# Background sums of a transformer-like layer, ordered behind the weight tile that precedes them in the transfer order

## The chip, the cores and the metric

The kernel runs as one program on one core of a Trainium2 chip. The metric is the device time of one execution in microseconds (us), as the median of three runs. The profile shows one execution engine by engine: PE is TensorE (matrix multiplication; PEld are its weight loads), DVE is VectorE, ACT is ScalarE, POOL is GpSimd, SP is SyncE, which here issues the large transfers. Each engine runs its own instructions strictly in the order in which they were built, and waits on semaphores for the others.

## The reference

One layer (DEPTH is 1) on 256 latent tokens of width 2048, with 256 context tokens, all in float32:

- `mod = silu(c) @ w_mod + b_mod` gives six rows of 2048: shift, scale and gate for each of two sub-layers. Context tokens use `silu(c_ctx)`.
- Token mixer: `h = modulate(rms_norm(x))`, one projection `h @ w_in` (11264 columns), a convolution branch, a gated recurrence with 8 heads in both directions, a projection of each branch, sigmoid gates, `w_out`, and `x + ga_m * rms_norm(y)`.
- MLP: `modulate(rms_norm(x))`, `square(relu(h @ w1)) @ w2` with 8192 hidden columns, and `x + ga_f * rms_norm(...)`.

What matters here: of `w_mod`, the first two rows (shift and scale of the mixer) are needed at once. The other four (the mixer's gate, shift and scale of the MLP, the MLP's gate) are needed much later, and the kernel computes them in the background, on VectorE rather than on TensorE.

## The kernel before

All weights come as tiles of 128 x 1024 float32 (512 KB). To keep float32 precision on TensorE, each weight tile is split into two parts: ScalarE writes `whi`, a rounded copy (line 119), and VectorE writes `wlo`, the rest (line 120). TensorE then multiplies `whi` and `wlo` with the split activations. A tile that is used this way is called a weight tile below; making `whi` and `wlo` is its preparation, and `wlo` is its second part.

The class `Stream` holds one list of all tiles in the order of use. `fetch` issues the transfers from SP, strictly in list order, into a rotation of five raw buffers (`RAWS`); the transfer of a tile waits until the tile that held its buffer has been read for the last time. `prepare` takes the next tile of the list. For a weight tile it allocates one of four pairs of `whi` and `wlo` (`AHEAD`) and makes the two parts; a pair comes free when TensorE has used it, so preparation runs at most four tiles ahead of TensorE.

Between weight tiles stand 128 background tiles, also of 512 KB, each with a function `fn`. `prepare` calls it and returns; such a tile has no `whi` or `wlo`. There are two kinds, and both are one VectorE instruction over the raw tile, called a sum below:

- `dots` (line 924), 64 tiles of `wmt`: multiplies the tile with the row `silu(c)` and adds up along the row.
- `gemv` (lines 909 and 911), 64 tiles of `wm1`: adds the tile, times one value per partition, to `gacc`. After 16 tiles the generator `gain_row` adds a bias (954), splits the result into `gpart` (231), lets TensorE add it up (966) and stores a gain row (968).

Where background tiles stand in the list: two behind each tile of the second half of the first context projection; one or two behind every second weight tile from there through the recurrence heads and the convolution's inputs; none behind the first 52 tiles of the gate projections, then one behind every fourth; one behind every second tile in the two branch projections (`who`, `wpw`) and in most of `wo`; one behind every sixth in the MLP.

Two things set the order on VectorE. The Python program is written in list order, and `pump` interleaves steps of background generators (the recurrence heads, the convolution). A scheduler then builds each engine's list from the program, by its own model of when an instruction's inputs are there; it may move an instruction past others that do not depend on it. `tc.issue_after(ins)` adds a constraint for that scheduler: what is recorded inside the block on the engine of `ins` stands behind `ins` in that engine's list. It adds no semaphore. The list `kn.los` holds the `wlo` instructions made so far, in list order.

A recurrence head runs through levels. On a level TensorE multiplies (1043) what ScalarE copied to `left` (1032), VectorE stores the result under a mask (`sc`, 1050), scales two halves of `x` (1058, 1059) and a decay tile `fg` (1061), and from these `left` is copied for the next level.

The projections called `tokens` (lines 253 to 255) work in groups: four banks of PSUM are filled over all weight tiles of the group, but the last three tiles (`LAST`) are taken bank by bank, so that the banks can be emptied one after the other. The three pairs of `whi` and `wlo` therefore come free almost together, at the end of the group. Emptying is lines 729 (`who`), 737 and 738 (`wpw`) on VectorE and 718 (gates) on ScalarE.

Of the kernel before, what the change touches and what calls it, by code (L numbers as in the profile page):

```python
# [49 lines left out]
class Stream:  # L50
# [49 lines left out]
    def prepare(self):  # L100
        self.fetch_to(1)
        ap, fn, paged = self.items[self.done]
        self.done += 1
        raw = self.raws.popleft()
        kn = self.kn
        nc = kn.nc
        if fn is not None:
            fn(raw)
            return
        if paged:  # L110
            hi, lo = (kn.page(F32R, "wpage")[:, :TW] for i in range(2))
        else:
            hi = kn.wp.tile([P, TW], F32R, name="whi", tag="whi", bufs=AHEAD)
            lo = kn.wp.tile([P, TW], F32R, name="wlo", tag="wlo", bufs=AHEAD)
        with ExitStack() as after:
            for ins in self.behind[0] if self.behind else ():
                after.enter_context(kn.tc.issue_after(ins.ins))
            self.behind = self.behind[1:]
            nc.scalar.activation(out=hi, in_=raw, func=AF.Copy)  # L119
            kn.los.append(nc.vector.tensor_tensor(lo, raw, hi.bitcast(F32), op=ALU.subtract))  # L120
        self.ready.append((hi, lo))
# [1148 lines left out]
```

## Time and profile before

| | us |
|---|---|
| median of 3 runs | 1670.3 |
| lowest, highest | 1669.09, 1670.92 |
| the profiled execution: its time | 1668.67 |
| its span | 1666.9 |
| PE busy in the span | 1628.6 |
| DVE busy | 1123.8 |
| ACT busy | 772.5 |

The span runs from the first to the last instruction of the program; the time of the execution is 1.77 us longer. Busy times of engines overlap. A row of a wait gives what waited, for whom, the sum, the number of times and the longest. A row of the timeline gives start, length, engine, line, operation, the tiles written and read, and in brackets the idle time before it and what ended it. In windows, each engine has its busy time and instruction count, and PEclk is the granted clock of TensorE as a share of full speed.

### The profile page before, as it was taken

What the parts mean: (1) busy time and instruction counts of PE and PEld (TensorE: products, weight loads), DVE (VectorE), ACT (ScalarE), POOL (GpSimd) and SP (SyncE); (2) the same over time, 40 slices, a digit from 0 to 9 for tenths busy, and PEclk for the clock granted to TensorE, in tenths of its full rate; (3) what the DMA queues carried; (4) which work ended last, traced back from release to release, by engine and by line L of the source; (5) the groups of instructions that cost most, each with busy time, mean ns of one, the idle gap of its engine ahead of it and who ended that gap; (6) DMA issues with size and microseconds to landing.
All of it is one profiled execution on the core that took longest, in us unless ns stands there. A gap on an engine that the chain in (4) does not pass through costs nothing.

```text
span 1666.9 us, 22131 instructions
## 1 busy us (share of the span) xinstructions
PE 1628.6 (98%) x8378; PEld 1366.7 (82%) x8378; DVE 1123.8 (67%) x1558; ACT 772.5 (46%) x1075; POOL 8.1 (0%) x18
## 2 busy tenths in 40 slices
PE   5999999999999999999999999999999999999997
PEld 3668888888888888778788898888888888888886
DVE  5446687887877888867887756456565665566555
ACT  4222444344554444643345655446543455345543
POOL 0000000000000000000000000000000000000000
PEclk9999999999999999999999999999999999999999
DMA  9997863543566555678888366677667666666553
GB/s 377 394 371 277 301 208 122 179 151 114 185 205 202 182 189 191 223 253 292 287 276 282 125 228 230 212 240 232 216 209 229 235 221 215 223 218 200 184 193 116
DMA packets 103338, 374.47 MB, mean 225 GB/s; under 512 B 11584, under 2 KB 11584, under 8 KB 103232
## 3 DMA queue, kind: packets, MB, share of 16 engines
q1 hardware_dynamic: 101952, 368.86, 65.1%
q0 software_dynamic: 1280, 4.21, 0.8%
q8 instruction: 65, 1.06, 0.3%
q14 instruction: 41, 0.34, 0.1%
HBM read 370.93 MB, written 2.10 MB: 224 GB/s over the span
## 4 chain that ended last, share of the span: by engine, by line
PE 81%; DVE 8%; DMA 6%; issue 2%; ACT 2%; SPq 0%; DVEq 0%; ACTq 0%
PE bank L179 19%; PE bank L246 18%; PE bank L255 10%; PE bank L254 10%; PE bank L253 10%; PE bank L248 9%; DMA raw<-wm 5%; DVE wlo L120 3%; PE bank L1043 2%; DVE gacc L911 1%; DMA raw<-wmt 1%; ACT whi L119 1%; DMA x<-ctx 1%; DVE raw L924 0%; ACT turned L891 0%
## 5 line engine op out<-in xcount | busy, mean ns | idle before, releaser
L120 DVE TENSOR_TENSOR wlo<-raw,whi 128x1024 fp32r<-128x1024 f32 x490 | 594.6, 1222 | 316.6 <-ACT whi L119 311.9
L119 ACT ACTIVATE whi<-raw 128x1024 fp32r<-128x1024 f32 x490 | 515.0, 1059 | 592.3 <-PE bank L255 304.8
L246 PE MATMUL bank<-h,whi 128*128 128x512 f32 x1280 | 322.2, 393 | 0.0
L246 PEld LDWEIGHTS bank<-h,whi 128*128 128x128 f32 x1280 | 230.3, 189 | 41.4
L179 PE MATMUL bank<-h,whi 128*128 128x512 f32 (+1 forms) x768 | 210.7, 362 | 1.8 <-ACT whi L119 1.0
L253 PE MATMUL bank<-whi,hidh 128*128 128x512 f32 x500 | 194.6, 389 | 0.0
L254 PE MATMUL bank<-wlo,hidh 128*128 128x512 f32 x500 | 194.6, 389 | 0.0
L255 PE MATMUL bank<-whi,hidl 128*128 128x512 f32 x500 | 194.5, 389 | 0.0
L248 PEld LDWEIGHTS bank<-h,wlo 128*128 128x128 f32 x1280 | 174.6, 190 | 12.6
L254 PE MATMUL bank<-wlo,h 128*128 128x512 f32 x448 | 175.6, 392 | 4.3 <-DVE wlo L120 4.2
L248 PE MATMUL bank<-h,wlo 128*128 128x256 f32 x1280 | 178.4, 282 | 0.0
L253 PE MATMUL bank<-whi,h 128*128 128x512 f32 x448 | 175.5, 392 | 0.0
L255 PE MATMUL bank<-whi,h 128*128 128x512 f32 x448 | 175.0, 391 | 0.0
L179 PEld LDWEIGHTS bank<-h,whi 128*128 128x128 f32 x768 | 132.1, 190 | 24.6 <-issue 5.9
L179 PE MATMUL bank<-h,wlo 128*128 128x512 f32 (+1 forms) x384 | 135.6, 355 | 0.0
L911 DVE SCALAR_TENSOR_TENSOR gacc<-raw,silu_c,gacc 128x1024 f32<-128x1024 f32 x60 | 77.0, 1283 | 66.4 <-DMA raw<-wm 66.4
L255 PEld LDWEIGHTS bank<-whi,hidl 128*128 128x128 f32 x500 | 93.8, 188 | 19.6
L254 PEld LDWEIGHTS bank<-wlo,hidh 128*128 128x128 f32 x500 | 93.9, 188 | 19.5
L253 PEld LDWEIGHTS bank<-whi,hidh 128*128 128x128 f32 x500 | 93.9, 188 | 19.2
L254 PEld LDWEIGHTS bank<-wlo,h 128*128 128x128 f32 x448 | 84.5, 189 | 23.3 <-DVE wlo L120 6.0
L255 PEld LDWEIGHTS bank<-whi,h 128*128 128x128 f32 x448 | 84.4, 188 | 17.6
L253 PEld LDWEIGHTS bank<-whi,h 128*128 128x128 f32 x448 | 84.5, 189 | 17.2
(206 smaller groups left out, 1617.7 us busy)
## 6 DMA issues: line engine op xcount, KB each, us to landing
raw<-w SPq DMA_DIRECT2D x256, 512.0 KB, 4.2
raw<-wi SPq DMA_DIRECT2D x172, 512.0 KB, 4.0
raw<-wm SPq DMA_DIRECT2D x80, 512.0 KB, 4.3
raw<-wmt SPq DMA_DIRECT2D x64, 512.0 KB, 4.2
rawpage<-wm SPq DMA_DIRECT2D x48, 512.0 KB, 9.2
raw<-wo SPq DMA_DIRECT2D x32, 512.0 KB, 4.7
raw<-who SPq DMA_DIRECT2D x16, 512.0 KB, 4.7
raw<-wpw SPq DMA_DIRECT2D x16, 512.0 KB, 5.1
```

Source lines behind the costliest of these rows:

```text
L119: nc.scalar.activation(out=hi, in_=raw, func=AF.Copy)
L120: kn.los.append(nc.vector.tensor_tensor(lo, raw, hi.bitcast(F32), op=ALU.subtract))
L179: ins = fn(*args, **kw)
L246: nc.tensor.matmul(bank, w[0][:, cut(i)], x(k)[2], start=(k == 0), stop=False)
L248: nc.tensor.matmul(bank[:, T:], w[1][:, cut(i)], x(k)[0], start=False, stop=(k == nk - 1))
L253: nc.tensor.matmul(out, x[0], w[0], start=first, stop=False)
L254: nc.tensor.matmul(out, x[0], w[1], start=False, stop=False)
L255: nc.tensor.matmul(out, x[1], w[0], start=False, stop=last)
L911: nc.vector.scalar_tensor_tensor(acc, raw, s, acc, op0=ALU.mult, op1=ALU.add)
L1043: nc.tensor.matmul(ps[:, b * P:(b + 1) * P], w, r, start=True, stop=True)
```

## The change

The call of a background tile's function is put into a block that orders it behind the last `wlo` made so far, that is, behind the second part of the weight tile that precedes it in the list. No instruction is added or taken away, and no size, buffer or transfer is changed. The file becomes two lines longer, so that line 120 is 122 after the change, 911 is 913, and so on.

```diff
@@ -105,7 +105,9 @@
         kn = self.kn
         nc = kn.nc
         if fn is not None:
-            fn(raw)
+
+            with kn.tc.issue_after(kn.los[-1].ins):
+                fn(raw)
             return
         if paged:
             hi, lo = (kn.page(F32R, "wpage")[:, :TW] for i in range(2))
```

The built programs show how this moves instructions. The first place is VectorE at the change from the projection `who` to `wpw`, where the group's four banks are emptied (`gate`). Before:

```order
L911 SCALAR_TENSOR_TENSOR gacc<-raw,silu_c,gacc 128x1024
L120 TENSOR_TENSOR wlo<-raw,whi 128x1024
L729 TENSOR_TENSOR gate<-bank,gate 128x512 x2
L911 SCALAR_TENSOR_TENSOR gacc<-raw,silu_c,gacc 128x1024
L729 TENSOR_TENSOR gate<-bank,gate 128x512
L120 TENSOR_TENSOR wlo<-raw,whi 128x1024 x2
L729 TENSOR_TENSOR gate<-bank,gate 128x512
L120 TENSOR_TENSOR wlo<-raw,whi 128x1024 x2
```

And with the change:

```order
L913 SCALAR_TENSOR_TENSOR gacc<-raw,silu_c,gacc 128x1024
L122 TENSOR_TENSOR wlo<-raw,whi 128x1024
L731 TENSOR_TENSOR gate<-bank,gate 128x512 x3
L122 TENSOR_TENSOR wlo<-raw,whi 128x1024
L913 SCALAR_TENSOR_TENSOR gacc<-raw,silu_c,gacc 128x1024
L122 TENSOR_TENSOR wlo<-raw,whi 128x1024
L731 TENSOR_TENSOR gate<-bank,gate 128x512
L122 TENSOR_TENSOR wlo<-raw,whi 128x1024
```

The sum that stood between the emptying of the second and the third bank now stands behind the first `wlo` that follows the third bank.

The second place is VectorE in the levels of the first recurrence head (its tile is `x_1824`). Before:

```order
L1061 TENSOR_TENSOR fg<-fg 128x256
L924 SCALAR_TENSOR_TENSOR raw,dot<-raw,silu_row 128x1024
L1050 COPY_PREDICATED sc<-masks,bank 128x2x128
L1058 TENSOR_TENSOR x_1824<-x_1824,fg 128x96x4
L1059 TENSOR_TENSOR x_1824<-x_1824,fg 128x96x4
L120 TENSOR_TENSOR wlo<-raw,whi 128x1024
L1061 TENSOR_TENSOR fg<-fg 128x128
L1010 TENSOR_SCALAR fg<-fg,lbm,lb 128x512
L1050 COPY_PREDICATED sc<-masks,bank 128x2x128
```

And with the change:

```order
L1063 TENSOR_TENSOR fg<-fg 128x256
L1052 COPY_PREDICATED sc<-masks,bank 128x2x128
L1060 TENSOR_TENSOR x_1824<-x_1824,fg 128x96x4
L1061 TENSOR_TENSOR x_1824<-x_1824,fg 128x96x4
L122 TENSOR_TENSOR wlo<-raw,whi 128x1024
L1063 TENSOR_TENSOR fg<-fg 128x128
L926 SCALAR_TENSOR_TENSOR raw,dot<-raw,silu_row 128x1024 x2
L1052 COPY_PREDICATED sc<-masks,bank 128x2x128
```

Sums that stood singly on several levels now stand as a pair behind a `wlo`. Counted over the whole of VectorE's two lists, 107 of the 128 sums stood ahead of the `wlo` of the weight tile before them, by one to four `wlo`; with the change none does, 124 stand right behind it and the first four one or two `wlo` later, where they stood before. The order on SP and POOL is unchanged. On TensorE a few small multiplications of the heads, of the gain rows and of the transposes ahead of `wo` move by one to six rows, and on ScalarE some copies change places with neighbours.

## The prediction

> **What bounds the kernel now.** I read the busy times first, then TensorE by stage, then who it waits for.
>
> ```profile
> span 1666.9 us, 22131 instructions
> PE 1628.6 (98%) x8378; PEld 1366.7 (82%) x8378; DVE 1123.8 (67%) x1558; ACT 772.5 (46%) x1075; POOL 8.1 (0%) x18
> ```
>
> TensorE is busy 1628.6 of 1666.9 us. The change gives it no less to do, so it can win only what TensorE loses: the 38.3 us in which it is idle, and time in which its clock is down. By stage (columns: length, then busy time of PE, PEld, DVE, ACT, POOL; clock; DMA share; GB/s):
>
> ```profile
> 200.00:480.00 280.00, 278.59 (x1545) 241.09 (x1544) 220.62 (x407) 121.56 (x227) 1.45 (x2) 1.00 0.50 166
> 680.00:960.00 280.00, 271.97 (x1290) 225.72 (x1288) 210.08 (x251) 142.56 (x209) 4.32 (x8) 0.99 0.73 248
> 960.00:1640.00 680.00, 679.96 (x3546) 585.03 (x3547) 403.41 (x404) 340.80 (x423) 2.09 (x4) 1.00 0.66 217
> ```
>
> The MLP (960 to 1640) has nothing to win: 0.04 us idle. The heads (200 to 480) have 1.41 us, and the stretch from the end of the gates to the end of `wo` (680 to 960) has 8.03 us and a clock below 1.00. The rest of the 38.3 lies in the start and the tail, where no sum moves. Who is waited for:
>
> ```profile
> PE bank L254 <- DVE wlo L120: 4.2, 3, 1.9
> PE bank L966 <- DVE gpart L231: 1.8, 2, 1.5
> PE bank L1043 <- ACT left L1032: 1.3, 3, 0.5
> ```
>
> ```profile
> DVE gacc L911 <- DMA raw<-wm: 66.4, 50, 3.7
> DVE raw L924 <- DMA raw<-wmt: 20.2, 18, 2.3
> ```
>
> VectorE stands 86.6 us in front of sums whose transfer has not landed. All that is behind such a sum waits too, though its own inputs may be there. That costs something only where TensorE is short of a `wlo`, and the first rows say where to look: three times, 4.2 us.
>
> **The change, part by part.** Nothing is added, so durations stay: a sum 1.28 us, a `wlo` 1.2, a `whi` 1.06. Only places on VectorE's list move.
>
> *First stall.* VectorE, ScalarE and TensorE around 742:
>
> ```profile
> 735.16 2.40 DVE L120 TENSOR_TENSOR wlo<-raw,whi 128x1024 fp32r<-128x1024 f32 x2
> 741.26 1.28 DVE L911 SCALAR_TENSOR_TENSOR gacc<-raw,silu_c,gacc 128x1024 f32<-128x1024 f32 x1 [3.70 <-DMA raw<-wm]
> 742.47 2.35 DVE L120 TENSOR_TENSOR wlo<-raw,whi 128x1024 fp32r<-128x1024 f32 x2
> ```
>
> ```profile
> 737.97 1.06 ACT L119 ACTIVATE whi<-raw 128x1024 fp32r<-128x1024 f32 x1 [1.66 <-PE bank L255]
> ```
>
> ```profile
> 741.62 0.39 PE L255 MATMUL bank<-whi,h 128*128 128x512 f32 x1
> 741.85 0.39 PE L253 MATMUL bank<-whi,h 128*128 128x512 f32 x1
> 743.74 0.50 PE L254 MATMUL bank<-wlo,h 128*128 128x512 f32 x1 [1.51 <-DVE wlo L120]
> ```
>
> Matmuls start every 0.23 us. The `whi` is ready at 739.03, but VectorE idles until 741.26 for a transfer of a tile that comes later in the list, sums until 742.47, and only then makes the `wlo`. With the sum behind it, that `wlo` runs from about 739.1 to 740.3, and TensorE asks for it at 742.08: 1.8 us to spare. The idle 1.5 us goes. **Term 1: -1.5** (no less, since the spare is larger than what moved things could cost here; at most 1.66, the step 741.85 to 743.74 less 0.23).
>
> *Second stall*, at the group end shown in the order rows:
>
> ```profile
> 791.16 1.22 DVE L120 TENSOR_TENSOR wlo<-raw,whi 128x1024 fp32r<-128x1024 f32 x1
> 792.29 1.28 DVE L729 TENSOR_TENSOR gate<-bank,gate 128x512 f32<-128x512 f32 x2
> 795.86 1.28 DVE L911 SCALAR_TENSOR_TENSOR gacc<-raw,silu_c,gacc 128x1024 f32<-128x1024 f32 x1 [2.29 <-DMA raw<-wm]
> 797.07 0.68 DVE L729 TENSOR_TENSOR gate<-bank,gate 128x512 f32<-128x512 f32 x1
> 797.67 2.35 DVE L120 TENSOR_TENSOR wlo<-raw,whi 128x1024 fp32r<-128x1024 f32 x2
> ```
>
> ```profile
> 792.81 2.96 ACT L119 ACTIVATE whi<-raw 128x1024 fp32r<-128x1024 f32 x3 [5.74 <-PE bank L255]
> ```
>
> ```profile
> 796.69 0.39 PE L253 MATMUL bank<-whi,h 128*128 128x512 f32 x1
> 798.94 0.64 PE L254 MATMUL bank<-wlo,h 128*128 128x512 f32 x1 [1.86 <-DVE wlo L120]
> ```
>
> Three pairs come free together, three `whi` follow back to back from 792.81, and their `wlo` are wanted at once. In the new order a third bank is emptied ahead of the `wlo`; it was waited for behind the sum before, so its own time is not seen. Banks end nine matmuls (2.1 us) apart and the three `whi` start when the tile is last read, about 1.4 us before the last bank ends, so bank three is out at most 0.7 us after 792.81; with its 0.68 the `wlo` still ends by 795.4, and TensorE asks at 796.92. The sum then comes between the first and the second `wlo`: the second ends by 795.4 + 1.28 + 1.2 = 797.9, while TensorE needs it 12 matmuls later, at 799.7. The fourth bank's emptying and the third `wlo` end by 799.8, against 802.4. **Term 2: -1.9** (0.7 if the third bank came 2.3 us later than I place it; 2.0 at most).
>
> *The clock behind it.* Windows of 2 us, same columns:
>
> ```profile
> 798.00:800.00 2.00, 1.06 (x3) 0.87 (x4) 2.00 (x3) 0.00 (x0) 0.00 (x0) 0.79 1.03 416
> 800.00:802.00 2.00, 2.00 (x7) 1.54 (x6) 2.00 (x4) 1.06 (x1) 0.00 (x0) 0.50 0.93 344
> 802.00:804.00 2.00, 2.00 (x9) 1.65 (x8) 0.89 (x1) 0.65 (x1) 0.00 (x0) 0.86 0.99 313
> ```
>
> The clock falls to half right behind the longest stall and is back by 804. Lost: 2 x (0.21 + 0.50 + 0.14) = 1.7 us. Nothing follows the shorter stall at 742. I take it that without the stall the clock stays: **term 3: -1.7** (0 if the drop has another cause). [...]
>
> *The third wait on a `wlo`*, at the end of the gates:
>
> ```profile
> 698.34 0.50 PE L254 MATMUL bank<-wlo,h 128*128 128x512 f32 x1 [0.88 <-DVE wlo L120]
> ```
>
> ```profile
> 690.54 1.22 DVE L924 SCALAR_TENSOR_TENSOR raw<-raw,silu_row 128x1024 f32<-128x1024 f32 x1 [0.96 <-DMA raw<-wmt]
> 692.84 1.74 DVE L333 RECIPROCAL lnmu<-lnmu 128x256 f32<-128x256 f32 x1
> ```
>
> From 690.54 VectorE has no pause until the late `wlo`. Taking the sum and its wait out of that run gives 2.2 us, and the new order has this sum behind the `wlo`; but the reciprocal waits for the convolution's own chain, which may not come earlier. Between 0 and -0.9, I take **term 4: -0.6**.
>
> *The gain row:*
>
> ```profile
> 830.16 0.51 PE L966 MATMUL bank<-gpart,ones_r 128*128 128x512 f32 x1 [1.45 <-DVE gpart L231]
> ```
>
> The chain sum, bias, split, matmul has the same length, its last sum is now later in VectorE's list, and TensorE's rows for it move one to three matmuls (0.2 to 0.7 us) later. TensorE itself arrives sooner. Between +0.7 and -1.4, **term 5: -0.4**.
>
> *The heads.* 20.2 us of waits for `wmt` go, which lie between levels. Against that, pairs of sums (2 x 1.22) now stand on one level. A level takes 12 matmuls and four small ones, about 3.2 us, and where VectorE is ahead it waits:
>
> ```profile
> 241.16 0.45 DVE L1050 COPY_PREDICATED sc<-masks,bank 128x256 f32<-128x256 uint8 x1 [1.09 <-PE bank L1043]
> 242.44 1.22 DVE L120 TENSOR_TENSOR wlo<-raw,whi 128x1024 fp32r<-128x1024 f32 x1
> ```
>
> The level's own work is 1.3 us (241.16 to 242.44) and `fg`, about 0.3. A level with two sums and a `wlo` is 1.6 + 2.4 + 1.2 = 5.2 us of VectorE: 2.0 too long, less that 1.1. By the order lists six levels are like that, three before, so up to 3 x 0.9 = +2.7; the other end is -1.3, all that line 1043 waits for. The ends nearly cancel: **term 6: 0**.
>
> *What a later sum holds up.* A raw buffer is freed later, and SP's next transfers with it.
>
> ```profile
> raw<-wm SPq DMA_DIRECT2D x80, 512.0 KB, 4.3
> raw<-wpw SPq DMA_DIRECT2D x16, 512.0 KB, 5.1
> ```
>
> With a sum behind every second tile, five buffers hold 3.3 weight tiles, 3.3 x 2.7 = 9 us of TensorE; transfer, `whi` and `wlo` take 5.1 + 1.1 + 1.2 = 7.4. **Term 7: 0**, as long as transfers stay under about 6.7 us.
>
> Sum: -1.5 - 1.9 - 1.7 - 0.6 - 0.4 = -6.1. The profiled execution took 1668.67 (span 1666.9), 1.6 below the median of 1670.3; I take the sum off the median: **1664.2 us**.
>
> **The rivals.**
>
> *A. As summed, in size or part:* terms 1 and 2 alone with the clock give 5.1; 1665.2. All at their best (1.66 + 2.0 + 1.7 + 0.9 + 1.4 + 1.3) give 9.0; 1661.3.
>
> *B. The heads and the gain row give it back:* terms 1 to 3 hold, but +2.7 and +0.7 come on top: -1.7, 1668.6. For it speaks that pairs of sums are new; against it that the waits on `wmt`, which no order of instructions shows, go away there.
>
> *C. The bubbles stay:* three pairs freed at once need 3 `whi` and 3 `wlo`, whatever the order, and only four pairs exist. Then terms 1 to 3 vanish, 1669.7 with term 4. [...] Against it: at 737.97 and 792.81 the `whi` were made in time, and the pair was free.
>
> *D. Slower: transfers come late.* From 720 to 920 each sum holds its buffer until the preceding `wlo` is done, so that at a group end the next transfers start after the burst. If they then take over about 6.7 us, TensorE runs dry at each of the six group ends, by about 2.0 us plus 1.7 of half clock: 6 x 3.7 less the 5.7 of terms 1 to 4 = +16.5, 1686.8. It decides from transfers of 6.7 us; 5.1 is the median there, and `x` is loaded beside them around 784 to 800.
>
> *E. The change does nothing:* excluded for most sums by the order lists (107 of 128 move), open only if VectorE's waits reappear in other places; 1670.3.
>
> **How the numbers follow.** Runs of this kernel differ by up to 1.8 us; what is within 0.2% (3.3 us) counts as no change. A 0.72, B 0.12, C 0.08, D 0.06, E 0.02. Faster means below 1667.0: nearly all of A, 0.71; slower is D, 0.06; the rest 0.23. The range holds A, with a run's spread at its lower end, and B with most of C up to 1669.3: 1660.3 to 1669.3; A's own is 1661 to 1667.
>
> **What would show it.** Right: the waits of the sums on DMA fall from 86.6 to under 15 us; the wait of line 254 (then 256) on `wlo` from 4.2 to under 0.5; the clock at 1.00 from 790 to 810; PE idle from 680 to 960 about 4 instead of 8.0 us. Terms 5 and 6 are read from the waits of the gain row's matmul and of the `left` level. It would be wrong if new waits of `whi` on `raw` appear between 720 and 920 (D), or if TensorE still waits for `wlo` at group ends with no sum in front (C).

## The result, and the profile after

The changed kernel takes 1659.85 us (median of 6 executions, 1658.71 to 1660.90), the kernel before beside it 1669.69 us (6 executions, 1667.99 to 1672.97). The ratio is 0.9941, with a 95% interval from 0.9931 to 0.9952: faster, by 0.6%. Measured again beside the last experiments, the ratio was 0.9932 (0.9915 to 0.9948); one execution of the kernel before, of 4227 us, is left out there. The forecast was 1664.2 us with a range from 1660.3 to 1669.3; the time lies 0.45 us under its lower end. The direction and the places were right, the size was too small. The profiled pair went from 1668.67 to 1659.94 us, its span from 1666.9 to 1658.2.

The same three stages as before, in the profile after; its program runs up to 8.7 us ahead, so that the same stretch of time holds slightly later work (length, then busy time of PE, PEld, DVE, ACT, POOL; clock; DMA share; GB/s):

```profile
200.00:480.00 280.00, 279.36 (x1550) 241.75 (x1550) 219.87 (x408) 122.05 (x227) 1.46 (x2) 1.00 0.50 165
680.00:960.00 280.00, 277.05 (x1355) 232.60 (x1354) 215.50 (x254) 146.59 (x213) 4.33 (x8) 1.00 0.72 253
960.00:1640.00 680.00, 680.00 (x3516) 583.79 (x3516) 399.92 (x402) 336.96 (x421) 2.10 (x4) 1.00 0.65 215
```

TensorE's idle time falls from 1.41 to 0.64 us in the heads and from 8.03 to 2.95 us between the gates and `wo`, and the clock there is 1.00 instead of 0.99. The MLP had nothing to win and won nothing. Who TensorE still waits for, of the rows that concern the change:

```profile
PE bank L968 <- ACT gpart L233: 1.0, 1, 1.0
PE bank L1045 <- ACT left L1034: 0.5, 1, 0.5
```

The row of line 256 and `wlo` (254 before, 4.2 us) is gone; one wait for a gain row and one for `left` remain. And the waits for transfers:

```profile
DVE raw L926 <- DMA raw<-wmt: 0.2, 1, 0.2
```

```profile
ACT whi L121 <- DMA raw<-wpw: 18.2, 10, 5.3
ACT whi L121 <- DMA raw<-wo: 15.4, 12, 3.9
ACT whi L121 <- DMA raw<-who: 15.1, 9, 2.7
ACT whi L121 <- DMA raw<-w: 8.6, 5, 2.4
```

VectorE's 86.6 us in front of sums are now 0.2. ScalarE has taken over part of it: for `wpw`, `wo`, `who` and `w` it waits 57.3 us in all, where these rows of the kernel before add up to 6.8:

```profile
ACT whi L119 <- DMA raw<-wo: 3.8, 3, 1.9
ACT whi L119 <- DMA raw<-who: 2.0, 1, 2.0
ACT whi L119 <- DMA raw<-w: 1.0, 1, 1.0
```

The transfers are not quicker (the median from issue to landing is 4.7 us for `wm` and 5.8 for `wpw`, against 4.3 and 5.1 before); the engine that meets them first has changed. ScalarE's wait shows no cost on TensorE, which waits for a `whi` once for 1.0 us in both kernels; my reading is that behind the wait stands the next `whi`, which comes later in the list anyway. VectorE's wait did cost at a few places, where a `wlo` whose tile had already landed stood behind the sum and TensorE wanted it (1.51 us in front of 743.74 and 1.86 us in front of 798.94 in the kernel before).

Where the time went, in the profiled pairs. I took the start of the n-th matmul in each trace, subtracted that of the kernel before, and read the difference at the boundaries of the stages (us; the last three columns are experiments, told below):

| stage, in the time of the kernel before | forecast | after | after, second profile | dots alone | gemv alone | two sums |
|---|---|---|---|---|---|---|
| start, to 215 | 0 | +0.1 | 0.0 | +1.9 | +0.5 | -0.4 |
| heads and convolution inputs, to 679 | 0 (term 6) | -1.0 | -1.0 | -1.0 | -0.1 | 0.0 |
| end of the gates, to 733 | -0.6 (term 4) | -1.1 | -1.1 | -1.1 | 0.0 | 0.0 |
| first stall, to 780 | -1.5 (term 1) | -1.8 | -1.8 | -0.4 | -1.8 | -1.8 |
| second stall and clock, to 823 | -3.6 (terms 2, 3) | -3.8 | -3.5 | +1.7 | -3.7 | -3.6 |
| gain rows, to 952 | -0.4 (term 5) | -1.1 | -1.3 | -0.1 | -0.8 | -0.7 |
| MLP and end | 0 | 0.0 | 0.0 | 0.0 | 0.0 | 0.0 |
| span | -6.1 | -8.7 | -8.8 | +0.9 | -5.8 | -6.5 |

The second profile is that of the run called "after, again" in the table of experiments. The start changes by chance: it lies between -1.3 and +1.9 us in the kernels whose start is the same, so its row is not an effect of the edits.

At the first stall VectorE's timeline of the changed kernel reads:

```profile
737.02 1.23 DVE L122 TENSOR_TENSOR wlo<-raw,whi 128x1024 fp32r<-128x1024 f32 x1 [1.50 <-ACT whi L121]
738.16 1.28 DVE L913 SCALAR_TENSOR_TENSOR gacc<-raw,silu_c,gacc 128x1024 f32<-128x1024 f32 x1
739.75 1.23 DVE L122 TENSOR_TENSOR wlo<-raw,whi 128x1024 fp32r<-128x1024 f32 x1 [0.30 <-ACT whi L121]
```

Each wait is now one on a `whi` that has just been made, and no sum waits. At the second:

```profile
790.06 1.23 DVE L122 TENSOR_TENSOR wlo<-raw,whi 128x1024 fp32r<-128x1024 f32 x1 [1.08 <-ACT whi L121]
791.21 1.28 DVE L913 SCALAR_TENSOR_TENSOR gacc<-raw,silu_c,gacc 128x1024 f32<-128x1024 f32 x1
792.40 1.22 DVE L122 TENSOR_TENSOR wlo<-raw,whi 128x1024 fp32r<-128x1024 f32 x1
793.54 0.68 DVE L731 TENSOR_TENSOR gate<-bank,gate 128x512 f32<-128x512 f32 x1
794.14 1.21 DVE L122 TENSOR_TENSOR wlo<-raw,whi 128x1024 fp32r<-128x1024 f32 x1
795.27 1.28 DVE L913 SCALAR_TENSOR_TENSOR gacc<-raw,silu_c,gacc 128x1024 f32<-128x1024 f32 x1
```

The group's three `wlo` and the sum between them run nearly without a break. TensorE is busy without a gap. The clock reads 1.00 from 38.97 us to 1653.47 us in this trace; the window in which it was 0.50 before:

```profile
800.00:802.00 2.00, 2.00 (x11) 1.65 (x10) 1.93 (x3) 0.52 (x2) 0.00 (x0) 1.00 0.91 311
```

### The profile page after: what moved, and what is told of

Same layout as the page of the kernel before. It is cut to its first block, busy times and chain, and to the rows that moved or that the text cites. A ratio compares the mean times of both kernels' runs of the same rounds, so it can differ in the third digit from the quotient of the medians.

```text
span 1658.2 us, 22135 instructions
## 1 busy us (share of the span) xinstructions
PE 1626.7 (98%) x8378; PEld 1366.0 (82%) x8378; DVE 1122.5 (68%) x1558; ACT 772.5 (47%) x1075; POOL 8.1 (0%) x18
## 4 chain that ended last, share of the span: by engine, by line
PE 92%; DMA 4%; ACT 2%; DVE 2%; issue 1%; SPq 0%; DVEq 0%; ACTq 0%
PE bank L181 19%; PE bank L248 18%; PE bank L257 14%; PE bank L256 14%; PE bank L255 14%; PE bank L250 9%; PE bank L1045 2%; DMA raw<-wpw 1%; ACT whi L121 1%; DMA rawpage<-wm 1%; DMA raw<-wf 1%; DMA x<-ctx 0%; DVE wlo L122 0%; ACT turned L893 0%; PE bank L1076 0%
## 5 line engine op out<-in xcount | busy, mean ns | idle before, releaser
L255 PE MATMUL bank<-whi,h 128*128 128x512 f32 x448 | 174.7, 391 | 0.0
L257 PE MATMUL bank<-whi,h 128*128 128x512 f32 x448 | 174.3, 390 | 0.0
L181 PE MATMUL bank<-whi,h 128*128 128x512 f32 x256 | 83.1, 400 | 3.2 <-ACT h L233 3.2
```

The source lines that it names most:

```text
L181: ins = fn(*args, **kw)
L255: nc.tensor.matmul(out, x[0], w[0], start=first, stop=False)
L257: nc.tensor.matmul(out, x[1], w[0], start=False, stop=last)
```

## The experiments

The theory: a sum that waits for its own transfer holds up what stands behind it in VectorE's list, and at two group ends that is the `wlo` which TensorE needs next; two instructions carry most of the gain. Against it stood rival C (too few buffers), rival D (transfers late), and the question of what the 64 `dots` are worth.

| kernel | us | before, beside it | ratio, 95% interval |
|---|---|---|---|
| dots alone ordered | 1669.38 | 1670.60 | 0.9982 (0.9967 to 0.9996) |
| gemv alone ordered | 1664.06 | 1670.60 | 0.9944 (0.9927 to 0.9961) |
| two sums ordered | 1664.33 | 1670.87 | 0.9958 (0.9941 to 0.9975) |
| before, six raw buffers | 1679.23 | 1670.60 | 1.0043 (1.0029 to 1.0056) |
| after, six raw buffers | 1665.47 | 1670.02 | 0.9966 (0.9956 to 0.9977) |
| after, four raw buffers | 1677.34 | 1670.60 | 1.0028 (1.0014 to 1.0041) |
| after, gain rows two steps later | 1671.83 | 1670.02 | 1.0011 (1.0002 to 1.0020) |
| order behind the last wlo but one | 1659.30 | 1670.02 | 0.9937 (0.9919 to 0.9954) |
| order behind the last but two | 1661.75 | 1670.87 | 0.9947 (0.9928 to 0.9966) |
| last but one, first gain row a step later | 1659.51 | 1670.87 | 0.9932 (0.9915 to 0.9948) |
| after, again | 1659.47 | 1670.87 | 0.9932 (0.9915 to 0.9948) |
| after, with pauses of TensorE (one execution) | 1736.42 | 1670.02 | none |

The ratio on record and its interval are taken over the single executions; the ratio lies up to 0.2% from the quotient of the two medians beside it (for the `gemv` alone that is 0.9961).

### Half of the change: dots alone, gemv alone

```diff
-            with kn.tc.issue_after(kn.los[-1].ins):
+            with kn.tc.issue_after(kn.los[-1].ins) if fn.__defaults__ and len(fn.__defaults__) == 2 else ExitStack():
```

> Only the sums of wmt (the dot products, which lie in the projections of the context, the recurrence heads and the gates up to about 700 us) are ordered behind the preceding wlo; the sums of wm1 stay free. If each place pays by itself, as the two traces read: the heads 0.9 us and the end of the gates 1.1 us, so about 2 us below the kernel before (ratio 0.9988), with the stalls at 742 and 797 and the clock drop still there. If the gain is one thing, that VectorE as a whole has less to wait for, these 64 of 128 sums bring nearer half of the 9.8 us, 0.997.

```diff
-            with kn.tc.issue_after(kn.los[-1].ins):
+            with kn.tc.issue_after(kn.los[-1].ins) if len(fn.__defaults__) == 3 else ExitStack():
```

> Only the sums of wm1 (from about 710 us on) are ordered; the dot products stay free. Place by place: the stall at 742 (1.8 us), the one at 797 with the clock (3.8) and the gain rows (1.1) go, about 6.7 us below the kernel before, ratio 0.996; waits of these sums on transfers near 0, those of the dot products still about 20 us. Half and half would be 0.997.

The two halves split by stage in the table above. Ordering the `dots` gives what the changed kernel gains in the heads and at the end of the gates (-2.1 us). Behind them it gains nothing, and in this profile loses 1.2: the `gemv` sums still wait 75.9 us, and TensorE still waits for `wlo` in the projections, in part at other places (1.04 us ahead of 774 where the kernel before has 1.51 ahead of 744, then 2.95 ahead of 800 and 1.10 ahead of 824). By the timed runs it is worth 0.04 to 0.33%. Ordering the `gemv` gives the two stalls, the clock and part of the gain rows, 0.4 to 0.7%.

With the `dots` alone the second stall is even longer, 2.95 us, and yet the clock stays. TensorE there:

```profile
796.71 0.39 PE L255 MATMUL bank<-whi,h 128*128 128x512 f32 x1
800.05 0.50 PE L256 MATMUL bank<-wlo,h 128*128 128x512 f32 x1 [2.95 <-DVE wlo L122]
```

I come back to this row under the clock.

### Two instructions of 128

```diff
-            fn(raw)
+            with kn.tc.issue_after(kn.los[-1].ins) if fn.__defaults__ in ((0, 3, 0), (0, 12, 0)) else ExitStack(): fn(raw)
```

> Only two of the 128 sums are ordered: those that VectorE waited in front of at 741 and 796 us. The other sums of the same accumulation follow them, so VectorE's list changes between about 740 and 830 us and nowhere else; the lists of ScalarE, GpSimd and SyncE are those of the kernel before. If the two stalls and the half clock behind the second are what these sums cost (terms 1 to 3), the two steps of 1.8 and 3.8 us go as in the changed kernel and nothing else: 4.5 to 6 us less than before, 1664 to 1666 us, ratio 0.9965 to 0.9975, and in the trace the heads (200 to 480) and the end of the gates (680 to 703) as before. If the gain needs the order of all sums (transfers start in step with the list), less than 2 us, ratio above 0.9985.

Measured: 1664.33 us, inside the first range by time; the ratio, 0.9958, is a little below the one expected. By stage the profile agrees: nothing in the heads, nothing at the end of the gates, -1.8 and -3.6 us at the two stalls. The windows of this kernel in the three stages from the end of the gates on:

```profile
680.00:705.00 25.00, 24.06 (x110) 19.51 (x109) 20.66 (x28) 17.30 (x24) 0.00 (x0) 1.00 0.67 214
705.00:760.00 55.00, 55.00 (x246) 45.52 (x245) 37.45 (x44) 29.77 (x42) 1.17 (x2) 1.00 0.73 251
760.00:812.00 52.00, 51.81 (x229) 42.56 (x229) 39.60 (x38) 18.37 (x18) 2.11 (x4) 1.00 0.91 337
```

The 0.94 us in front of the late `wlo` at the end of the gates is still there (first row), the stalls at 742 and 797 are not. The sums still wait for transfers, 53.4 us for `wm` and 18.8 for `wmt`. So the waits of the sums are not themselves the cost: 72 of 86.6 us may stay, if those two do not stand in front of a `wlo` that is wanted. Terms 1 to 3 are shown by this run. Two sums were ordered, but eleven moved: nine neighbours between 741 and 814 us add to the same `gacc` and follow them, by one to three `wlo`.

### Buffers instead of order

```diff
-NPAGE = 30
+NPAGE = 29
-RAWS = 5
-FETCH = 13
+RAWS = 6
+FETCH = 14
```

Once in the kernel before, once in the changed one:

> The old order with six raw buffers instead of five (and 29 pages instead of 30 to make room; one more transfer is issued ahead at the start). If the bubbles come from too few buffers, a sixth lets transfers run one tile further ahead and the sums' waits on transfers fall well below 86 us, the time to about 1663. If they come from the order, the scheduler moves the sums one wlo further ahead with the sixth buffer (its list shows 45 of them four wlo ahead and 13 five), the sums still wait for their transfers, and the time stays within 2 us of the kernel before.

> The new order with six raw buffers (and 29 pages). If transfers are in time with five, nothing changes: 1659 to 1661. In the new order whi waits 18 us for wpw, 15 for wo and 15 for who, against 0 to 4 before; a sixth buffer should take most of these waits away, and if they cost TensorE anything the time falls below 1659.

A sixth raw buffer does not help the kernel before, it makes it slower. Its waits:

```profile
PE bank L254 <- DVE wlo L120: 6.6, 10, 1.4
```

```profile
DVE gacc L911 <- DMA raw<-wm: 84.1, 53, 4.7
DVE raw L924 <- DMA raw<-wmt: 23.5, 18, 4.3
```

The sums wait 107.6 us instead of 86.6, and TensorE ten times for a `wlo` instead of three. Most of the 0.43% is lost elsewhere: at 90 us TensorE stops for 3.64 us and the clock halves for 6.8 us, presumably since this edit also takes a page away and lengthens the prefetch; the changed kernel with six buffers has the same stop (3.64 us at 90 us) and loses 6 us there too. So the two are to be compared with one another: 0.9966 against 1.0043, a ratio of 0.9923. The order is worth as much with six buffers as with five, and more raw buffers do not replace it. No run added pairs of `whi` and `wlo`, which rival C had named; C falls by the run with two ordered sums, where both stalls are gone with the same four pairs.

```diff
-RAWS = 5
-FETCH = 13
+RAWS = 4
+FETCH = 12
```

> The new order with four raw buffers instead of five. By the margin worked out in the prediction, four buffers hold 2.7 weight tiles, 7.3 us of TensorE, where transfer, whi and wlo take 7.4: TensorE should run short of a tile at the group ends between 720 and 920 us and wait for whi on transfers, some 5 to 20 us slower than the new order with five, 1665 to 1680. If a held buffer costs nothing because transfers run far ahead, the time stays at about 1660.

With four buffers the changed kernel is slower than the kernel before. ScalarE's waits:

```profile
ACT whi L121 <- DMA raw<-wi: 56.5, 31, 5.4
ACT whi L121 <- DMA raw<-w: 40.3, 24, 3.7
ACT whi L121 <- DMA raw<-wo: 28.1, 20, 4.9
```

The trace is 14.8 us longer than that of the changed kernel: 6.5 us are lost before 215 us, in the start, and 7.8 us between 763 and 915, where the `gemv` sums stand and TensorE now waits for `wlo` seven times and for `whi` twice (4.8 us). The clock stays at 1.00 there. This is rival D, at about half its price, and one buffer away. With five, the margin of term 7 holds, though the 57.3 us of waits say that it is used.

### How far ahead a sum may stand

```diff
-            with kn.tc.issue_after(kn.los[-1].ins):
+            with kn.tc.issue_after(kn.los[-2].ins):
```

> The sums are ordered behind the wlo before the last one, so each may stand one wlo ahead of the new place (99 of 128 do, by the list). If what costs is that a wlo waits behind a transfer that comes later in the list, some of the waits come back: sums wait 20 to 50 us in all, and the time lies between, 1661 to 1665. If one wlo ahead is still hidden by the four pairs, it is as fast as the new order, 1660.

One `wlo` further ahead costs nothing: 1659.30 us. The sums wait 11.6 us in this kernel, less than I expected, and ScalarE's waits for `wpw`, `wo` and `who` are 20.5 us, against 48.7 in the changed kernel. With `kn.los[-3]`:

> Each sum is ordered behind the wlo three tiles before instead of the last one, which lets the scheduler put sums up to two wlo earlier. If what counts is only that no sum stands in front of a wlo whose transfer comes before its own by more than VectorE's slack, some waits of the sums on transfers return (15 to 40 us in sum) and the time stays within 2 us of the changed kernel, 1658 to 1662. If the place behind the preceding wlo is itself needed, the stalls at group ends return and the time is 1663 to 1668.

1661.75 us, inside the first range near its upper end, and 2.3 above the changed kernel on the same chip, a little more than the 2 us expected; the two intervals overlap. The sums wait 33.2 us (31.8 for `wm`, 1.4 for `wmt`). In its profile 1.3 us are lost in the start, and behind the start it gains 8.7 us, as much as the changed kernel (8.8). So the place behind the very last `wlo` is not needed. The kernel before, whose sums run ahead by up to four, has the stalls; three alone was not run.

### The gain rows

```diff
         yield None
         yield None
+        yield None
+        yield None
         row = self.grow[i, h] = self.page(F32, "gain_row")[:, :TW]
```

> The new order, with the four small matmuls of a gain row recorded two steps of the background pump later. In the new order's trace TensorE waits 1.0 us for gpart at 820 us. With two more steps (two weight tiles, 5.4 us) gpart is there, so about 1 us less than the new order, 1658.9; no gain if the wait only moves to another place.

The wait of the first gain row is gone, as meant, but the kernel loses about 12 us at another place:

```profile
PE bank L876 <- DVE y L799: 6.8, 1, 6.8
```

The multiplications of the second row now run at 925.74, and what the last step of `wo` makes of it on VectorE is wanted at once by TensorE's next transposes. From 930.73, inside the stop, the clock is at half for 17 us:

```profile
930.73:934.15 3.42, 0.55 (x3) 0.55 (x4) 2.67 (x8) 2.88 (x9) 0.00 (x0) 0.50 0.00 0
934.15:947.80 13.65, 13.65 (x65) 13.30 (x63) 6.53 (x14) 4.14 (x12) 0.00 (x0) 0.50 0.12 38
```

Only the first row, by one step, together with the order one ahead:

```diff
+        if (i, h) == (0, 0):
+            yield None
         row = self.grow[i, h] = self.page(F32, "gain_row")[:, :TW]
```

> Sums one wlo ahead, and the matmuls of the first gain row alone written one step of its generator later. In the changed kernel TensorE waits 1.0 us for this row at 820 us. If it is only written too early, the 1.0 us goes and nothing is late behind it, since the forced end of this row at the end of its group is one wlo away: 1657.5 to 1659.5, about 0.8 us under the changed kernel. If it comes too late as both rows did when two steps were added, the wait moves to the group end: 1663 to 1672, with a wait of 3 to 7 us behind 820.

The wait of this row is gone from the trace, and a wait of 0.6 us for a `wlo` at 804 is new. The 0.8 us that I expected are not there: the time, 1659.51 us, is that of the changed kernel beside it (1659.47):

> The changed kernel beside the three others on one chip: 1659 to 1661 us, ratio to before 0.993 to 0.995. Its spread should stay near 2 us where the kernel before spreads over 7 us and more, if the second stall of the kernel before costs the clock in some executions and not in others.

None of the versions beats the changed kernel by an amount that these runs can tell.

### The clock

The same kernel with 18 pauses in the MLP: TensorE's list gets a small multiplication, and then a transpose of a tile that GpSimd fills in one to eight steps first. It is added work; nothing of the computation is left out.

```diff
+        with self.tc.issue_after(behind.ins):
+            ps = self.bank()
+            nc.tensor.matmul(ps[:, :P], self.ones_r, self.ones_r, start=True, stop=True)
+        nc.scalar.copy(out=self.held[:, :P], in_=ps[:, :P])
+        for _ in range(times):
+            nc.gpsimd.memset(self.held[:, :cols], 1.0)
+        with self.tc.issue_after(behind.ins):
+            return nc.tensor.transpose(out=ps[:, :P], in_=self.held[:, :P], identity=self.v["ident"])
```

> The new order, and in the down projections of the first three quarters of the MLP eighteen added pauses of TensorE: a small matmul, a copy of its result on ScalarE, one to eight memsets on POOL, and a transpose for which TensorE waits. The pauses should last about 1 to 6 us. If the clock falls after a pause of some 2 us, as at 797 in the kernel before, pauses from about 2 us on are followed by 3.4 us at half clock, and those below about 1.7 us are not. If only a pause of a whole 3.4 us or more does it, those of 2 to 3 us keep the clock at 1.00, and the drop at 799 had another cause.

Seventeen of the pauses came out between 1.50 and 5.04 us; at the other one TensorE waited for a gain row instead (0.57 and 0.84 us). Length alone does not sort them: after one of 2.67 us the clock halved, after one of 3.62 us it did not, and after another of 3.62 us it did. What sorts them is a grid. In the kernel before, the half clock at 799.14 begins 764.58 us after the one at the start (34.56), and that is 224.00 times 3.4133 us; it lasts 3.413 us, one step. In the kernel with pauses every half clock up to 1540 us begins a whole number of such steps behind the first (352, 357, 369, 378, ...), and in all 14 traces it lasts 1, 2 or 5 whole steps, the one at the very end of a program aside. So I cut the traces on this grid. Windows of the kernel with pauses, in pairs: a window with a pause, and the one behind it (the second number is TensorE's busy time, the one ahead of the last two the clock):

```profile
1250.10:1253.51 3.41, 1.10 (x6) 0.93 (x7) 1.90 (x2) 0.00 (x0) 2.08 (x4) 1.00 0.68 229
1253.51:1256.92 3.41, 3.41 (x10) 2.65 (x9) 0.00 (x0) 0.00 (x0) 0.00 (x0) 0.50 0.53 198
```

```profile
1437.83:1441.24 3.41, 1.43 (x8) 1.16 (x8) 1.23 (x1) 1.21 (x2) 0.62 (x2) 1.00 0.89 284
1441.24:1444.65 3.41, 3.41 (x10) 2.65 (x9) 0.00 (x0) 0.29 (x1) 0.00 (x0) 0.50 0.45 157
```

```profile
1263.75:1267.16 3.41, 1.58 (x8) 1.12 (x6) 1.92 (x2) 1.21 (x2) 0.53 (x2) 1.00 0.70 261
1267.16:1270.58 3.42, 1.64 (x8) 1.39 (x9) 0.46 (x1) 0.00 (x0) 1.55 (x4) 1.00 0.53 177
```

The first two windows are idle for 2.31 and 1.98 us, and half clock follows. The first pause of 3.62 us is cut into 1.84 and 1.78, and none follows; the second has 2.94 us in one window. The stall of 2.95 us with the `dots` alone is cut in the same way:

```profile
795.50:798.92 3.42, 1.59 (x8) 0.98 (x6) 1.95 (x3) 0.28 (x1) 0.00 (x0) 1.00 0.80 231
798.92:802.33 3.41, 2.28 (x10) 1.87 (x11) 3.41 (x4) 0.26 (x1) 0.00 (x0) 1.00 1.03 363
802.33:805.74 3.41, 3.41 (x17) 2.81 (x16) 2.17 (x3) 1.86 (x2) 0.00 (x0) 1.00 0.91 342
```

And the kernel before, whose second stall lay wholly in one window:

```profile
795.73:799.14 3.41, 1.55 (x7) 0.97 (x7) 3.28 (x4) 0.04 (x1) 0.00 (x0) 1.00 0.84 302
799.14:802.56 3.42, 3.42 (x9) 2.67 (x9) 3.42 (x4) 1.06 (x1) 0.00 (x0) 0.50 0.96 356
```

Over the 14 traces, between the start and the tail, all 11 windows at full clock with at least 1.98 us of idle time are followed by half clock, and 29 of 30 with 1.0 to 1.84 us are not. Between them lie the 1.86 of the kernel before, with half clock, and a 1.92 without. The exception is a window of the kernel with pauses that was idle for 1.44 us (from 1233.03) and is followed by half clock; it is the one with the two waits for a gain row, and I have no explanation for it. So in these traces the boundary lies near 1.9 us of 3.41, somewhat over half a window. Eight of the 11 windows are from the one kernel with pauses.

## Why the prediction was too small

**Terms 1 to 3 were right.** They were forecast at -5.1 and measured -5.6 (-1.8 and -3.8). The kernel with two ordered sums shows that the place of these two is the cause. The 0.5 is arithmetic: I took idle times from the bracket, but a matmul takes 0.39 us where the next one starts after 0.23, so a stop costs 0.16 more than the idle time in front of the next matmul, and the matmul that ends it is followed after 0.34 instead of 0.23 us (743.74 to 744.08). The steps between starts had shown most of it (1.66 for the first stall, which I kept only as the upper bound).

**Term 3** (-1.7) held in the profiled pair. The other branch of the expectation for the kernel with pauses, that only a pause of a whole 3.4 us or more costs the clock, is not what the runs showed: a window of 3.41 us with 1.98 us of idle time was followed by half clock. But the row alone said less than I took from it: the 1.86 us of the kernel before lie between 1.84 and 1.92 that cost nothing elsewhere, and neither did the 2.95 us of the `dots` kernel. The windows begin 0.42 us past a whole number of steps from the program's first instruction in the trace of the kernel before, and 1.42 us in that of the changed kernel. I infer from it that whether an execution of the kernel before pays the 1.7 us depends on where a window begins; one execution of it was profiled, and it paid.

**Term 4** (-0.6) was mis-sized: -1.1. I had kept half for the reciprocal, which might not come earlier. It did come earlier (690.83 against 692.84, of which 0.9 is the gain of the heads), the sum now stands behind the first of the two late `wlo`, and the whole stop of 0.88 + 0.16 us is gone.

**Term 5** (-0.4) was mis-sized: -1.1 to -1.3, near the end of its bounds that I called -1.4. The longer of the first row's waits fell from 1.45 to 0.98 us, and the wait of 0.31 us before the second row, at 919.95, disappeared, with the 0.16 that a stop costs besides.

**Term 6** (0) is the step that failed in its reasoning. I counted up to +2.7 for levels with two sums, and let it cancel the gain. The changed kernel has such levels. VectorE, at the first of them:

```profile
235.70 1.22 DVE L122 TENSOR_TENSOR wlo<-raw,whi 128x1024 fp32r<-128x1024 f32 x1
236.84 0.39 DVE L1063 TENSOR_TENSOR fg<-fg 128x128 f32<-128x128 f32 x1
237.15 1.21 DVE L926 SCALAR_TENSOR_TENSOR raw<-raw,silu_row 128x1024 f32<-128x1024 f32 x1
238.29 1.22 DVE L926 SCALAR_TENSOR_TENSOR raw<-raw,silu_row 128x1024 f32<-128x1024 f32 x1
239.44 0.43 DVE L1052 COPY_PREDICATED sc<-masks,bank 128x256 f32<-128x256 uint8 x1
```

and TensorE's small multiplications of the levels around it:

```profile
236.97 0.60 PE L1045 MATMUL bank<-x,left 128*128 128x128 f32 x4
241.52 0.71 PE L1045 MATMUL bank<-x,left 128*128 128x128 f32 x4
244.39 0.64 PE L1045 MATMUL bank<-x,left 128*128 128x128 f32 x4
246.97 0.71 PE L1045 MATMUL bank<-x,left 128*128 128x128 f32 x4
```

The level with the pair takes 4.55 us where 3.2 was the rule, so the pair does stretch it, as I had reckoned. But TensorE does not stop for it: the scheduler builds all lists from one program, and it put 18 matmuls of the projection ahead of this level's multiplications, and 10 and 8 ahead of the next two (2.87 and 2.58 us), where 12 stood ahead of each before. I had read on the order rows that a few small multiplications move, and then costed the pair as if TensorE's list had stayed. At none of the other levels with a pair does TensorE stop either: in the heads one wait of 0.49 us, at 469.79, is left of four. What remained was the good end, -1.0 of the -1.3 for `left`, and the kernel with the `dots` alone shows the same -1.0.

**Term 7** (0) held: no transfer came too late for TensorE. But the sign that I had named for rival D, new waits of `whi` on `raw` between 720 and 920, did appear (48.7 us for `wpw`, `wo` and `who`, against 5.8 before) without its cost. It was a bad sign to name: ScalarE's idle time is not TensorE's. The sign of D is TensorE's wait for `whi` or `wlo`, and with four buffers it was there.

**From the sum to the median.** The terms come from one execution that lay 1.6 us under its median, and I took them off the median. With the measured -8.7 that gives 1661.6, and 1659.85 was measured: 1.7 us more. Of this, 0.6 is the median that I started from: three more executions of the kernel before brought it from 1670.3 to 1669.69. The profiled execution of the changed kernel lies at its median (1659.94 and 1659.85). For the other 1.1, a typical execution of the kernel before loses more than its profiled one, and the change seems to take that away too: 62 executions of the kernel before, beside the experiments, spread from 1667.0 to 1679.1 us, 12 of the changed kernel from 1658.2 to 1661.6. The slowest quarter of the 62 has a mean clock of 0.9950, the fastest 0.9962, which fits stalls that cost the clock in some executions and not in others. But this difference is worth about 2 us (0.0012 of 1667), and the two quarters lie 6.6 us apart; what makes the rest stays open. The miss of 4.35 us is thus 2.6 us of terms, above all 6 (1.0), 5 and 4, and 1.7 us of this.

The rivals: A is what happened; the 8.7 us of the profile lie inside its best case of 9.0, and the time lies beyond it only because of the last point. B, C and E are excluded by the profile after and the experiments. D is one raw buffer away.

## What to carry to other kernels

An engine that runs its list in order, as VectorE does here (86.6 us in front of sums before, 0.2 after), should not wait for something late in front of something early: place background work behind the urgent instruction that precedes it in the order of the transfers, and look for the few places where the urgent one is wanted next, since ordering two instructions of 128 carried most of this gain (5.4 of 8.7 us). The scheduler that saw the change re-placed TensorE's work too (18, 10 and 8 matmuls ahead of the multiplications of three levels, where 12 stood), so a cost on one engine may not be charged as if the others' lists had stayed. Sum losses by the steps between starts, and compare the profiled execution with the spread of the runs before taking a sum off the median.

## What the runs showed of the hardware

Half clock of TensorE came and went in whole steps of 3.413 us on a grid (224.00 steps between the two half clocks of the kernel before), and the idle time of one window went with the clock of the next: 1.98 us in one window were followed by half clock, a pause of 3.62 us that was cut into 1.84 and 1.78 was not. I had not expected the second from the row.

Half clock outlasted the pause by four windows in one trace. After the stop of 6.8 us with the late gain rows, TensorE was busy for 13.65 of 13.65 us and still had half the clock for all four windows of them. In these windows 63 matmuls start, 50 of them the small multiplications of ones by ones that line 901 of that kernel issues ahead of the MLP, the other 13 transposes. The second and the third window hold ones alone, 16 each. The clock came back behind the fourth window, which holds eight transposes and the last seven of the ones:

```profile
944.39:947.80 3.41, 3.41 (x17) 3.06 (x16) 0.00 (x0) 1.12 (x3) 0.00 (x0) 0.50 0.10 40
947.80:951.21 3.41, 3.21 (x28) 3.16 (x28) 2.69 (x4) 3.41 (x6) 0.00 (x0) 1.00 0.02 5
```

In the changed kernel the same 50 run at full clock, and it stays:

```profile
929.86:933.27 3.41, 3.41 (x33) 3.41 (x32) 2.62 (x4) 3.15 (x9) 0.00 (x0) 1.00 0.00 0
```

So the clock stayed at 1.00 through these multiplications of ones where it was full, and two windows of them alone did not bring it back where it was 0.50. Three windows that read as busy (3.41 of 3.41 us) were each followed by half clock, and only the fourth by full clock. What brings the clock back is open: this is one stop in one trace, and no run separated it.
